# Hybrid streaming layer: where the HGRN mixer's diagonal products stand, and gates that read PSUM directly

## The chip, the cores and the metric

One core of a Trainium2 chip runs the whole kernel. The metric is the device time of one execution in microseconds. The core's engines work side by side, each with its own queue in order: TensorE (PE) multiplies matrices into PSUM, VectorE (DVE) and ScalarE (ACT) read PSUM and SBUF, GpSimd (POOL) works on SBUF only in this kernel, and SyncE (SP) issues nearly all DMA transfers. An instruction that waits holds up everything behind it in its queue.

## What is computed

One layer of a streaming encoder: RMSNorm, one input projection, three mixers on its columns (RG-LRU, SSD, HGRN), an output projection, and a SwiGLU block, for 1152 rows (1024 of a prompt, 8 x 16 of running streams). The change touches the HGRN mixer, the gate of the SSD mixer and the projections that feed both. Cut to these:

```python
h = rmsnorm(x, p["norm1_w"])                       # a scale per row, times a weight per column
proj = jnp.einsum("btd,de->bte", h, p["w_in"])     # ..., z, ..., q, fpre, ig, og

def ssd_mixer(z, ...):
    v = (y.reshape(b_, t, B_WIDTH) * jax.nn.silu(z)).reshape(b_, t, B_GROUPS, -1)
    v = v * lax.rsqrt(jnp.mean(v * v, axis=-1, keepdims=True) + EPS)
    return v.reshape(b_, t, B_WIDTH) * norm_w

def hgrn_chunk(s, inp):
    q, lf, k, v = inp
    bc = jnp.cumsum(lf, axis=1)
    decay = jnp.exp(jnp.where(causal_mask, bc[:, :, None] - bc[:, None], -jnp.inf))
    att = jnp.einsum("bthk,bshk,btshk->bths", q, k, decay)
    o = jnp.einsum("bths,bshv->bthv", att, v) + jnp.einsum("bthk,bhkv->bthv", q * jnp.exp(bc), s)
    ...

def hgrn_mixer(q, fpre, ig, og, s0, lb, norm_w):
    q = jax.nn.silu(q)
    ...
    o = o * lax.rsqrt(jnp.mean(o * o, axis=-1, keepdims=True) + EPS) * norm_w
    return o * jax.nn.silu(og), s_t
```

On the diagonal of `att` (t = s) the decay is 1, so that entry is the sum over k of q times k, per head.

## The kernel before

The rows are nine tiles of 128 (`NT`), in three chunks of 384 (`NCHUNK`). The projections take the normalised input without its row scale: the scale `rstd1` (per row, as a column) or `rrow` (the same as a row) is multiplied in when a result leaves PSUM. Every fp32 product is made of three matmuls (`mm3`, lines 144 to 146) of a high and a low half, so a tile of a projection with eight steps of depth is 24 matmuls. Channel-major projections (`ch_tile`: `f0`, `f1`, `q0`, `q1` and those of the other mixers) give tiles of 128 x 384; row-major ones (`tok_piece`: `v` with `dt`, the output gate `og`, the gate `z`) give 128 x 264 or 128 x 256 for each of the nine row tiles.

PSUM has eight banks in four tags: `a` 2, `b` 2, `c` 3, `d` 1. Row-major projections use tag `a`; `v` alternates between `a` and `b`. A bank is taken again when its last reader is through.

In `proj_f` and `proj_q` the HGRN mixer's inputs are made for both channel halves j: `bc` is the running sum of log f (a scan on DVE, line 415), `ct` is exp of the key's logarithm, and `kb` keeps `ct` and exp(bc). With q ready, `bc` becomes exp(bc) times q (line 430) and goes to DRAM (`qkbd`), and `ct` becomes k times q (line 433), from which nine small matmuls with the head selector `hsel` (128 x 2) make the diagonal `pd`, copied to `dia` (line 437). `mix_c` reads `dia` when it makes the output of a row tile, and reads the rest back from `qkbd` as `ldq`; `W` are its decay weights. The softplus of `dt` (`spt`) has one power on POOL (line 636).

A gate (`proj_gate`) is a copy of PSUM to SBUF with the row scale on ACT (line 458), a tanh of that on ACT (459), and a product on DVE (460): sg (1 + tanh(sg / 2)), which is 2 silu. It is written to DRAM and read back by the mixers. The factor 1/2 is put back through `hnw` (line 859) for `og` and in `mix_b` (line 766) for `z`.

Program order in the code is `first_tiles` (f0, f1, q0), `proj_f`, `proj_q(0)`, `proj_vdt`, `proj_q(1)`, `proj_og`, `ssd_steps`, the nine `mix_c`, then the other mixers. It isn't the order on the engines: a scheduler places the instructions of every engine by its own estimate of times, with priorities (`feed()` goes ahead by 3000), and so the matmuls of different tiles mix. Each engine then runs its list in order. Names in the rows below have the tile's number behind them, as in `ptv_4`.

Of the kernel before, what the change touches and what calls it, by code (L numbers as in the profile page):

```python
# [11 lines left out]
F32 = mybir.dt.float32  # L12
# [3 lines left out]
AF = mybir.ActivationFunctionType  # L16
ALU = mybir.AluOpType

P = 128
# [5 lines left out]
NT = NCHUNK * TPC  # L25
# [65 lines left out]
def hybrid_step(ctx, tc, xT, xTp, vec, rows, nrow, wch, wtk0, wtk1, wout, wgate, wup, wdown,  # L91
# [3 lines left out]
    V, S, G, T = nc.vector, nc.scalar, nc.gpsimd, nc.tensor  # L95
# [29 lines left out]
    rstd1 = cp.tile([P, NT], F32, name="rstd1")  # L125
    rrow = cp.tile([P, NTOK], F32, name="rrow")

    def bank(tag, name, shape):
        n = int(np.prod(shape))
        t = ps.tile([P, 512], F32, tag=tag, name=name, bufs=PB[tag])  # L130
        v = t[:, 0:n]
        if len(shape) == 2:
            v = v.rearrange("p (a b) -> p a b", b=shape[1])
        elif len(shape) == 3:
            v = v.rearrange("p (a b c) -> p a b c", b=shape[1], c=shape[2])
        return v

    def mm(out, lhsT, rhs, start=True, stop=True):
        T.matmul(out, lhsT, rhs, start=start, stop=stop)
# [34 lines left out]
    def rstd_from(out, ss, n):  # L174
        V.tensor_scalar(out, ss, 1.0 / n, EPS, ALU.mult, ALU.add)
        powc(out, out, 0)
# [5 lines left out]
    pr = p1.__enter__()  # L182
# [5 lines left out]
    hnw = pr.tile([P, 2], F32, name="hnw")  # L188
    seqm = cm[:, M_SEQ:M_SEQ + NB]
    hsel = cm[:, M_HS:M_HS + 2]  # L190
    dtb, dsk = rw[:, 0:8], rw[:, 16:24]
    st = {}
# [82 lines left out]
    def first_tiles(names, ws):  # L275

        outs = [stile(name) for name in names]
        for c in range(NCHUNK):
            hT, cs = st["hT", c], slice(c * CH, (c + 1) * CH)
            for name, w, out in zip(names, ws, outs):  # L280
                pm = bank("aabbccc"[pcount[0] % 7], f"pm{name}_{c}", [CH])
                pcount[0] += 1
                for k in range(KD):
                    mm3(pm, wk(w, k, P), (hT[:, 0, k, :], hT[:, 1, k, :]), k == 0, k == KD - 1)
                with feed():
                    if name == "q0":
                        V.scalar_tensor_tensor(out[:, cs], pm, 0.5, rrow[:, cs], ALU.mult, ALU.mult)
                    else:
                        V.tensor_tensor(out[:, cs], pm, rrow[:, cs], ALU.mult)
        return outs  # L290
# [132 lines left out]
    def proj_q(j, q):  # L423

        th = pr.tile([P, NB * 19 + 3 + 1024], F32, tag="raw", name=f"th{j}")[:, 0:NTOK]
        S.activation(th, q, AF.Tanh)
        V.scalar_tensor_tensor(q, th, 1.0, q, ALU.add, ALU.mult)
        to_tiles(qkbd[:, :, j * P:(j + 1) * P], q)
        k, eb = st["kb", j]
        V.tensor_tensor(eb, eb, q, ALU.mult)  # L430
        to_tiles(qkbd[:, :, (6 + j) * P:(7 + j) * P], eb)

        V.tensor_tensor(k, k, q, ALU.mult)
        pd = bank("b", f"pd{j}", [NT, 2])
        for t in range(NT):
            mm(pd[:, t, :], k[:, t * P:(t + 1) * P], hsel)
        V.tensor_copy(dia[:, :, 2 * j:2 * j + 2], pd)

    def proj_vdt():
        w = [load_w(wtk0[h], 1056, f"t0{h}") for h in range(2)]  # L440
# [11 lines left out]
    def proj_gate(w, name, dst, ts=range(NT)):  # L452

        for t, pm in tok_piece(w, 256, name, ts):
            sg = pr.tile([P, 256], F32, tag="stg", name=f"gs{name}{t}", bufs=2)
            th = pr.tile([P, 256], F32, tag="th", name=f"th{name}{t}", bufs=2)
            with feed():
                S.activation(sg, pm, AF.Copy, scale=rstd1[:, t:t + 1])
                S.activation(th, sg, AF.Tanh, scale=0.5)
                V.scalar_tensor_tensor(sg, th, 1.0, sg, ALU.add, ALU.mult)  # L460
                dma(dst[t], sg)

    def proj_og():
        w = [load_w(wtk1[2, h], 1024, f"t3{h}") for h in range(2)]
        proj_gate(w, "og", vod[:, :, 256:512])
# [21 lines left out]
    def mix_c(t):  # L487
# [80 lines left out]
        for h in range(4):  # L568
            j, r = h // 2, (h % 2) * 64
# [25 lines left out]
        else:  # L595
            pn = bank("c", f"pnc_{t}", [2, 64])
            for h in range(4):
                j, r = h // 2, (h % 2) * 64
# [13 lines left out]
        ss = pr.tile([P, 1], F32, tag="ssc", name=f"ssc{t}", bufs=2)  # L612
        S.activation(ke.rearrange("p j s -> p (j s)"), of, AF.Square, accum_out=ss)
        rstd_from(ss, ss, 256)
        V.scalar_tensor_tensor(of, of, ss, og, ALU.mult, ALU.mult)
        pm = bank("d", f"pmc{t}", [2, P])
        for j in range(2):
# [59 lines left out]
    def mix_b(t, last):  # L677
# [12 lines left out]
        zt = wk6[1][:, 0:512]  # L690
# [72 lines left out]
            G.tensor_tensor(yv, yv, xq, ALU.add)  # L763
        V.tensor_tensor(yv, yv, py, ALU.add)
        yf = yv.rearrange("p h d -> p (h d)")
        V.scalar_tensor_tensor(yf, yf, 0.5, zt, ALU.mult, ALU.mult)
        ss = pr.tile([P, 2], F32, tag="ssb", name=f"ssb{t}", bufs=2)
        jk = xq.rearrange("p h d -> p (h d)")
        for g in range(2):
# [86 lines left out]

    V.tensor_scalar(vc[:, V_CWB:V_CBB + 8], vc[:, V_CWB:V_CBB + 8], 0.5, None, ALU.mult)

    V.tensor_scalar(hnw, hnw, 0.5, None, ALU.mult)
    cvp = pr.tile([P, 10, 3], F32, name="cvp")  # L860
    h0t = pr.tile([P, 2, NB], F32, name="h0t")
    dma(h0t, h0)
# [24 lines left out]
    for a in zw:  # L887
        G.memset(a, 0.0)
    dtr = pr.tile([P, NH], F32, name="dtr")
    sml = pr.tile([P, 6, NH], F32, name="sml")  # L890
    etb = pr.tile([P, NB, 8], F32, name="etb")


    f0, f1, q0 = first_tiles(("f0", "f1", "q0"), ws)
    proj_f((f0, f1))
    proj_q(0, q0)
    proj_vdt()
    proj_q(1, plain_tile(13, "q1"))
    proj_og()
    ssd_steps()  # L900
    for t in range(NT):
        mix_c(t)
# [528 lines left out]
```

## Time and profile before

| | us |
|---|---|
| three runs, median (lowest to highest) | 1468.39 (1464.24 to 1470.4) |
| profiled execution | 1464.5 |
| its span, first to last instruction | 1462.7 |
| PE busy | 1364.8 |
| DVE busy | 1084.1 |
| ACT busy | 533.3 |
| POOL busy | 516.9 |

The profile is one execution. The profiled one is 3.9 us below the median of the three runs. An engine's busy time counts the time in which it has an instruction at work; what it does not count are its waits, and those of PE, the fullest engine, are the ones to look for.

### The profile page before, as it was taken

To read this page: it belongs to the slowest core of one execution; us is meant where nothing else is said; L and a number is where in the kernel's file an instruction comes from. 1 tells how busy PE (TensorE), PEld (TensorE's weight loads), DVE (VectorE), ACT (ScalarE), POOL (GpSimd) and SP (SyncE) were. 2 spreads that over 40 slices of the span, in tenths; PEclk is the share of its full clock that TensorE was granted. 3 is DMA by queue.
4 is the path that set the end of the run, shared out by engine and by line. 5 is a ranking of instruction groups with operands and counts; after the bars stand their busy time and mean duration, and the time that the engine had idled before them with its cause. 6 is when DMAs were issued, how large, how long until landed. Compare 5 with 4: busy or idle time off the path is not lost.

```text
span 1462.7 us, 24412 instructions
## 1 busy us (share of the span) xinstructions
PE 1364.8 (93%) x9341; PEld 1312.8 (90%) x9341; DVE 1084.1 (74%) x2010; ACT 533.3 (36%) x922; POOL 516.9 (35%) x417
## 2 busy tenths in 40 slices
PE   8879998999999899878799999999999999999986
PEld 7879887899988788778799999999999999998985
DVE  8555588987779588698646665556756688999996
ACT  7323265444543244364322312322222363333322
POOL 4213032100014322213644545445545432543453
PEclk9989999999999899998899999999999999999999
DMA  6245123332447686851323222233231454544523
GB/s 234 79 140 164 41 74 97 109 108 91 146 159 270 215 287 223 282 169 60 129 81 115 101 101 77 72 111 115 88 113 52 141 175 130 177 141 118 177 65 130
DMA packets 107289, 195.82 MB, mean 134 GB/s; under 512 B 10844, under 2 KB 66596, under 8 KB 107044
## 3 DMA queue, kind: packets, MB, share of 16 engines
q1 hardware_dynamic: 102276, 186.40, 38.8%
q0 software_dynamic: 4896, 7.87, 1.9%
q8 instruction: 73, 1.20, 0.3%
q14 instruction: 44, 0.36, 0.1%
HBM read 137.82 MB, written 56.41 MB: 133 GB/s over the span
## 4 chain that ended last, share of the span: by engine, by line
PE 40%; DVE 7%; DMA 1%; issue 1%; ACT 1%; POOL 0%; DVEq 0%; POOLq 0%; ACTq 0%
PE pd L146 3%; PE pd L144 3%; PE pd L145 3%; PE pS_g L144 3%; PE pS_u L144 3%; PE pS_g L146 3%; PE pS_u L145 3%; PE pS_g L145 3%; PE pS_u L146 3%; PE pA_u L144 2%; PE pA_u L146 2%; PE pA_u L145 2%; PE pA_g L145 2%; PE pA_g L144 2%; PE pA_g L146 2%; DVE as L180 1%
## 5 line engine op out<-in xcount | busy, mean ns | idle before, releaser
L144 PE MATMUL pd<-e,as 128*128 128x256 f32 (+1 forms) x560 | 167.6, 301 | 8.3 <-ACT as L179 4.9
L146 PE MATMUL pd<-e,as 128*128 128x256 f32 (+1 forms) x560 | 162.7, 298 | 3.0 <-DVE as L180 3.0
L145 PE MATMUL pd<-e,as 128*128 128x256 f32 (+1 forms) x560 | 165.1, 296 | 0.0
L144 PEld LDWEIGHTS pd<-e,as 128*128 128x128 f32 x560 | 106.5, 190 | 12.6 <-ACT as L179 6.4
L180 POOL TENSOR_TENSOR al_u<-wr_u,ah_u 128x1024 fp32r<-128x1024 f32 x30 | 72.1, 2403 | 117.0 <-ACT ah_u L179 117.0
L146 PEld LDWEIGHTS pd<-e,as 128*128 128x128 f32 x560 | 105.3, 190 | 4.7 <-DVE as L180 4.7
L145 PEld LDWEIGHTS pd<-e,as 128*128 128x128 f32 x560 | 106.1, 190 | 0.0
L180 POOL TENSOR_TENSOR al_g<-wr_g,ah_g 128x1024 fp32r<-128x1024 f32 x30 | 71.9, 2399 | 88.5 <-ACT ah_g L179 87.8
L179 ACT ACTIVATE ah_g<-wr_g 128x1024 fp32r<-128x1024 f32 x30 | 31.8, 1062 | 148.9 <-PE pS_u L145 80.5
L1040 POOL TENSOR_TENSOR g<-g,pt_u 128x256 f32<-128x256 f32 (+1 forms) x80 | 76.7, 976 | 20.3 <-DVE pt_u L1039 15.4
L144 PE MATMUL pw<-mT,wh_o 128*128 128x384 f32 x192 | 68.9, 362 | 8.3 <-DMA mT<-mixd 3.8
L144 PE MATMUL pS_g<-b,ah_g 128*128 128x256 f32 (+1 forms) x240 | 70.9, 296 | 2.1 <-ACT ah_g L179 2.1
L144 PE MATMUL pA_u<-b,ah_u 128*128 128x256 f32 (+1 forms) x240 | 71.0, 296 | 0.0
L145 PE MATMUL pA_g<-b,ah_g 128*128 128x256 f32 (+1 forms) x240 | 70.9, 296 | 0.0
L144 PE MATMUL pA_g<-b,ah_g 128*128 128x256 f32 (+1 forms) x240 | 70.8, 295 | 0.0
L146 PE MATMUL pA_u<-b,al_u 128*128 128x256 f32 (+1 forms) x240 | 70.8, 295 | 0.0
L146 PE MATMUL pA_g<-b,al_g 128*128 128x256 f32 (+1 forms) x240 | 70.7, 295 | 0.0
L144 PE MATMUL pS_u<-b,ah_u 128*128 128x256 f32 (+1 forms) x240 | 70.6, 295 | 0.0
L145 PE MATMUL pA_u<-b,ah_u 128*128 128x256 f32 (+1 forms) x240 | 70.6, 294 | 0.0
L145 PE MATMUL pS_g<-b,ah_g 128*128 128x256 f32 (+1 forms) x240 | 70.6, 295 | 0.0
L146 PE MATMUL pS_u<-b,al_u 128*128 128x256 f32 (+1 forms) x240 | 70.5, 294 | 0.0
L145 PE MATMUL pS_u<-b,ah_u 128*128 128x256 f32 (+1 forms) x240 | 70.4, 294 | 0.0
(726 smaller groups left out, 4810.7 us busy)
## 6 DMA issues: line engine op xcount, KB each, us to landing
wr_o<-in_dram SPq DMA_DIRECT2D x24, 512.0 KB, 4.8
wr_g<-in_dram SPq DMA_DIRECT2D x20, 512.0 KB, 3.5
wr_u<-in_dram SPq DMA_DIRECT2D x20, 512.0 KB, 3.5
wd<-in_dram SPq DMA_DIRECT2D x15, 512.0 KB, 3.9
wr_t<-in_dram SPq DMA_DIRECT2D x14, 512.0 KB, 3.7
fr<-ffd SPq DMA_DIRECT2D x11, 640.0 KB, 4.8
ffd<-g SPq DMA_DIRECT2D x10, 640.0 KB, 3.1
ffd<-g SPq DMA_DIRECT2D x10, 512.0 KB, 2.9
```

What stands on the lines that cost most here:

```text
L144: T.matmul(out, ah, bh, start=start, stop=False)
L145: T.matmul(out, ah, bl, start=False, stop=False)
L146: T.matmul(out, al, bh, start=False, stop=stop)
L179: S.activation(dst_hi, src, AF.Copy)
L180: eng.tensor_tensor(dst_lo, src, dst_hi.bitcast(F32), ALU.subtract)
L1040: G.tensor_tensor(g, g, u, ALU.mult)
```

## The change

Three things are changed. First, the diagonals: `proj_q` no longer makes them; a new function `diagonals`, called behind `proj_og`, makes all eighteen small matmuls into one bank and copies them once. In `proj_q` the product of k and q is now written ahead of the product of exp(bc) and q, and the latter goes from DVE to POOL. Second, the gates: ACT's tanh reads PSUM with half the row scale (`hr1` = `rstd1` / 2), and DVE multiplies 1 + tanh by PSUM itself. What is stored lacks the row scale. Third, the mixers bring it in: `mix_c` multiplies its own row factor `ss` by `hr1`, and `mix_b` uses `hr1` where 0.5 stood; the halving of `hnw` goes.

```diff
         k, eb = st["kb", j]
-        V.tensor_tensor(eb, eb, q, ALU.mult)
+        V.tensor_tensor(k, k, q, ALU.mult)
+        G.tensor_tensor(eb, eb, q, ALU.mult)
         to_tiles(qkbd[:, :, (6 + j) * P:(7 + j) * P], eb)
 
-        V.tensor_tensor(k, k, q, ALU.mult)
-        pd = bank("b", f"pd{j}", [NT, 2])
-        for t in range(NT):
-            mm(pd[:, t, :], k[:, t * P:(t + 1) * P], hsel)
-        V.tensor_copy(dia[:, :, 2 * j:2 * j + 2], pd)
+    def diagonals():
+
+        pd = bank("b", "pdia", [2, NT, 2])
+        for j in range(2):
+            k = st["kb", j][0]
+            for t in range(NT):
+                mm(pd[:, j, t, :], k[:, t * P:(t + 1) * P], hsel)
+        V.tensor_copy(dia.rearrange("p t (j r) -> p j t r", j=2), pd)
...
             with feed():
-                S.activation(sg, pm, AF.Copy, scale=rstd1[:, t:t + 1])
-                S.activation(th, sg, AF.Tanh, scale=0.5)
-                V.scalar_tensor_tensor(sg, th, 1.0, sg, ALU.add, ALU.mult)
+                S.activation(th, pm, AF.Tanh, scale=hr1[:, t:t + 1])
+                V.scalar_tensor_tensor(sg, th, 1.0, pm, ALU.add, ALU.mult)
                 dma(dst[t], sg)
...
         rstd_from(ss, ss, 256)
+        V.tensor_tensor(ss, ss, hr1[:, t:t + 1], ALU.mult)
         V.scalar_tensor_tensor(of, of, ss, og, ALU.mult, ALU.mult)
...
-        V.scalar_tensor_tensor(yf, yf, 0.5, zt, ALU.mult, ALU.mult)
+        V.scalar_tensor_tensor(yf, yf, hr1[:, t:t + 1], zt, ALU.mult, ALU.mult)
...
-    V.tensor_scalar(hnw, hnw, 0.5, None, ALU.mult)
...
+    V.tensor_scalar(hr1, rstd1, 0.5, None, ALU.mult)
     proj_f((f0, f1))
     proj_q(0, q0)
     proj_vdt()
     proj_q(1, plain_tile(13, "q1"))
     proj_og()
+    diagonals()
     ssd_steps()
```

The scheduler makes a new order of it. On PE, ahead of the first diagonals before (`ptv` are the tiles of v):

```order
L145 MATMUL ptv_4_729<-wl_t01_609,hT1_163 128x264
L146 MATMUL ptv_4_729<-wh_t01_608,hT1_163 128x264
L139 MATMUL pd0_590<-cm_91,ct0_553 128x2 x9
L144 MATMUL ptv_1_642<-wh_t00_602,hT0_104 128x264
L145 MATMUL ptv_1_642<-wl_t00_603,hT0_104 128x264
```

and where PE's list goes on behind `q0` now:

```order
L145 MATMUL pmq0_2_527<-hT2_206,wh_q0_137 128x384
L146 MATMUL pmq0_2_527<-hT2_206,wl_q0_138 128x384
L144 MATMUL ptv_1_632<-wh_t00_592,hT0_104 128x264
L145 MATMUL ptv_1_632<-wl_t00_593,hT0_104 128x264
L146 MATMUL ptv_1_632<-wh_t00_592,hT0_104 128x264
```

`ptv_1` stood behind `pd0`; it now follows `q0` at once, ahead of `q1`'s third chunk, and `pdia` follows in six pieces between the tiles of the output gate, from behind `ptog_1` to behind `ptog_8`.

On DVE, around the gates 3 to 5 of the output gate, before:

```order
L671 TENSOR_TENSOR dab_1302<-sml_314,cm_91 128x64
L460 SCALAR_TENSOR_TENSOR gsog3_1107<-thog3_1108,gsog3_1107 128x256
L536 TENSOR_TENSOR qw0_306<-W0_1_1321,ldq0_302 128x256 x2
L460 SCALAR_TENSOR_TENSOR gsog4_1138<-thog4_1139,gsog4_1138 128x256
L460 SCALAR_TENSOR_TENSOR gsog5_1169<-thog5_1170,gsog5_1169 128x256
```

and now:

```order
L463 SCALAR_TENSOR_TENSOR gsog3_1083<-thog3_1084,ptog_3_1058 128x256
L531 TENSOR_TENSOR W0_0_1302<-ldq0_301 128x16x8
L532 TENSOR_TENSOR W0_0_1302<-ldq0_301 128x16x8
L531 TENSOR_TENSOR W0_1_1311<-ldq0_301 128x32x4
L532 TENSOR_TENSOR W0_1_1311<-ldq0_301 128x32x4
L531 TENSOR_TENSOR W0_1_1311<-ldq0_301 128x64x2
L532 TENSOR_TENSOR W0_1_1311<-ldq0_301 128x64x2
L556 TENSOR_TENSOR ke0_1335<-ldq0_301 128x256
L577 COPY zw0_308<-ldq0_301 128x16
L577 COPY zw1_309<-ldq0_301 128x16
L463 SCALAR_TENSOR_TENSOR gsog4_1113<-thog4_1114,ptog_4_1088 128x256
```

The instructions that read `ldq0` stood two gates earlier; gate 4 is now behind them. What `ldq0` needs is made on POOL, whose list reads now (`spt1` is the power of the softplus):

```order
L412 TENSOR_TENSOR f1_317<-ct1_555,f1_317 128x1152
L431 TENSOR_TENSOR bc0_568<-bc0_568,q0_318 128x1152
L640 TENSOR_TENSOR spt1_1258<-cst_82,spt1_1258 128x72
L431 TENSOR_TENSOR bc1_577<-bc1_577,q1_864 128x1152
L323 COPY rawxa0_2336<-cvs_259 128x8x3
```

The two products with q are new there, one on either side of the power.

On DVE in the z stage, around the gate of row tile 7 (`px3`, `pB3`, `px0` are products of `mix_b` on PE, made behind `ptz0_8`), before:

```order
L766 SCALAR_TENSOR_TENSOR wb3_3_4432<-wb3_3_4432,wb3_1_4430 128x512
L164 TENSOR_TENSOR wl_o00_4807<-wr_o00_4805,wh_o00_4806 128x1024
L730 COPY zw0_309<-ws_4282 128x2x16
L460 SCALAR_TENSOR_TENSOR gsz07_4136<-thz07_4137,gsz07_4136 128x256
L730 COPY zw1_310<-ws_4282 128x2x16
```

and now:

```order
L463 SCALAR_TENSOR_TENSOR gsz06_4092<-thz06_4093,ptz0_6_4067 128x256
L778 SCALAR_TENSOR_TENSOR ws_4263<-ws_4263,ssb2_4387,nwr_94 128x256 x2
L180 TENSOR_TENSOR ws_4263<-pmb2_4394,ws_4263 128x512
L705 TENSOR_TENSOR wb3_3_4413<-px3_4420,sml_314 128x512
L706 TENSOR_TENSOR wb3_3_4413<-px3_4420,rw_93 128x512
L716 TENSOR_TENSOR wb3_4_4414<-pB3_4428,cm_91 128x256
L705 TENSOR_TENSOR ws_4263<-px0_4487,sml_314 128x512
L706 TENSOR_TENSOR ws_4263<-px0_4487,rw_93 128x512
L721 TENSOR_SCALAR wb3_2_4412<-wb3_2_4412,sml_314 128x128 x4
L463 SCALAR_TENSOR_TENSOR gsz07_4122<-thz07_4123,ptz0_7_4097 128x256
```

The gate comes earlier in the list than before, but it is now the last reader of its PSUM bank, where ACT's copy was.

## Rows read from the trace of the kernel before

**Rows 1.** The page: span, then busy time, share and instructions of each engine.

```profile
span 1462.7 us, 24412 instructions
PE 1364.8 (93%) x9341; PEld 1312.8 (90%) x9341; DVE 1084.1 (74%) x2010; ACT 533.3 (36%) x922; POOL 516.9 (35%) x417
```

**Rows 2.** PE's waits, whole span: us in total, times, longest.

```profile
PE pd L139 <- DVE ct L433: 9.1, 1, 9.1
...
PE pmq L144 <- ACT wh_q L160: 1.0, 1, 1.0
```

**Rows 3.** Timeline of PE, 57 to 114 us: start, duration, line, operands, idle before.

```profile
57.32 0.34 PE L146 MATMUL pmq<-hT,wl_q 128*128 128x384 f32 x1
...
64.02 0.28 PE L144 MATMUL ptv<-wh_t,hT 128*128 128x264 f32 x1
...
72.62 0.28 PE L146 MATMUL ptv<-wh_t,hT 128*128 128x264 f32 x1
81.95 4.00 PE L139 MATMUL pd<-cm,ct 128*128 128x2 f32 x18 [9.05 <-DVE ct L433]
...
105.47 0.34 PE L144 MATMUL pmq<-hT,wh_q 128*128 128x384 f32 x1
...
113.89 0.28 PE L144 MATMUL ptog<-wh_t,hT 128*128 128x256 f32 x1
```

**Rows 4.** Stretches 82 to 101.5 us: busy of each engine, granted clock, DMA.

```profile
82.00:86.00 4.00, 4.00 (x19) 4.00 (x20) 3.96 (x3) 0.00 (x0) 0.00 (x0) 0.50 0.92 251
86.00:90.50 4.50, 4.50 (x21) 4.50 (x22) 1.70 (x3) 1.72 (x2) 0.00 (x0) 0.50 0.90 246
90.50:101.50 11.00, 11.00 (x93) 11.00 (x92) 3.25 (x10) 0.61 (x1) 0.00 (x0) 1.00 0.41 133
```

**Rows 5.** Timeline of DVE, 71 to 86 us.

```profile
71.71 4.99 DVE L415 TENSOR_TENSOR_SCAN bc<-rst,ct 128x1152 f32<-128x1152 f32 x1
...
81.86 1.36 DVE L430 TENSOR_TENSOR bc<-bc,q 128x1152 f32<-128x1152 f32 x1
83.25 2.56 DVE L415 TENSOR_TENSOR_SCAN bc<-rst,ct 128x1152 f32<-128x1152 f32 x1
```

**Rows 6.** Timeline of POOL, three products and powers between 70 and 204 us.

```profile
70.61 8.51 POOL L412 TENSOR_TENSOR f<-ct,f 128x1152 f32<-128x1152 f32 x2 [12.46 <-DVE ct L411]
...
108.65 11.84 POOL L636 TENSOR_TENSOR spt<-cst,spt 128x72 f32<-128x72 f32 x1 [29.54 <-DVE spt L635]
...
200.50 2.70 POOL L382 TENSOR_TENSOR g<-g,ga 128x1152 f32<-128x1152 f32 x1 [0.96 <-DVE g L381]
```

**Rows 7.** Output gate: tile ptog (ns min/median/max, first and last start), timelines of PE, SyncE, DVE.

```profile
L146 PE MATMUL ptog<-wh_t,hT x72: 277/280/365, 114.1 to 141.6; 128*128 128x256 f32 x72
...
122.98 2.07 PE L139 MATMUL pd<-cm,ct 128*128 128x2 f32 x18
...
118.92 0.63 SPq L395 DMA_DIRECT2D qkbd<-bc  x1
...
127.88 0.29 DVE L528 TENSOR_TENSOR W<-ldq 128x128 f32<-128x128 f32 x1 [0.37 <-DMA ldq<-qkbd]
...
191.86 0.14 DVE L175 TENSOR_SCALAR ssc<-ssc 128x1 f32<-128x1 f32 x1
```

**Rows 8.** z stage: a stretch, DVE's gates grouped, and timelines of ACT and DVE.

```profile
413.00:488.00 75.00, 67.31 (x467) 61.64 (x466) 63.41 (x135) 30.40 (x67) 26.05 (x24) 0.95 0.62 209
...
L460 DVE SCALAR_TENSOR_TENSOR gsz<-thz,gsz x18: 407/417/1491, 386.9 to 489.7; 128x256 f32<-128x256 f32 x18
...
445.84 0.46 ACT L458 ACTIVATE gsz<-ptz,rstd 128x256 f32<-128x256 f32 x1
...
469.30 0.47 ACT L458 ACTIVATE gsz<-ptz,rstd 128x256 f32<-128x256 f32 x1
...
451.22 1.26 DVE L460 SCALAR_TENSOR_TENSOR gsz<-thz,gsz 128x256 f32<-128x256 f32 x1
...
475.38 0.41 DVE L460 SCALAR_TENSOR_TENSOR gsz<-thz,gsz 128x256 f32<-128x256 f32 x1
```

More of the change, by code (lines that the diff above doesn't have):

```diff
@@ L889, in hybrid_step @@
     dtr = pr.tile([P, NH], F32, name="dtr")
+    hr1 = pr.tile([P, NT], F32, name="hr1")
     sml = pr.tile([P, 6, NH], F32, name="sml")
```

## The prediction

> **What bounds the kernel now.** I read the page's busy table first, to see which engine is nearly full, then the waits of TensorE (PE), then the timelines of the longest wait. PE is busy for 1364.8 of 1462.7 us, 93%, and VectorE (DVE) for 74% [rows 1]. So time is won where PE stands still or runs slowly, and an edit on ScalarE (ACT, 36%) wins nothing by itself. Sorted by length, PE's waits begin with a single one of 9.1 us: `pd`, the diagonal products, waits for DVE's line 433, the product of `ct` and `q` [rows 2]. PE's timeline shows it: the last `ptv` matmul is issued at 72.62, `pd` starts at 81.95, after 9.05 us without work [rows 3]. The next `ptv` matmuls could have run then, since their weights and inputs lay ready, but they are behind `pd` in PE's queue. The stall is paid a second time: from 82 to 90.5 us the granted clock is 0.50, the lower level (1.2 GHz), and 1.00 in the stretch behind it [rows 4].
>
> **The change, part by part.**
>
> 1. Both diagonals go behind the output gate's projection. This removes the 9.05 us. It takes the first group of `pd` off the slow stretch: 18 records took 4.00 us there [rows 3] and 2.07 us at the full clock at 123 us [rows 7]; they come back later at 2.07, so 1.93 is won. In 86 to 90.5 us 21 matmuls took 4.5 us where the next stretch runs 93 in 11.0, or 0.118 each [rows 4]; 21 × 0.118 = 2.5, so 2.0 is won. The bank that `pd0` held is free, so the order puts `ptv_1` and the start of `ptv_3` in front of `q1`, where PE waited 1.0 for `wh_q` [rows 2]: 1.0 won. Sum 9.05 + 1.93 + 2.0 + 1.0 = 14.0 us.
>
> 2. What is late next in that stretch. One `ptv` tile takes (72.74 − 64.02) / 3 = 2.91 us and one `q` tile (113.89 − 105.47) / 2 = 4.21 [rows 3]. From 57.5, the end of `q0`, nine `ptv` and three `q` tiles are 26.2 + 12.6 = 38.8, with about 0.8 for the broadcast `prr`; the output gate could start at 97.1 instead of 113.89. But `ptv_6` needs the bank that `vs2` empties, and DVE does that behind the scan of `bc0`, which took 4.99 us beside POOL's line 412 and ended at 76.7 [rows 5, 6]. In the new order `prr` comes some 2.4 us later, and the DVE chain with it: `vs2` ends near 80, PE arrives at 79.6. I take 0.5 us lost, between 0 and 1.5. A little later `q1`'s second tile needs the bank that `vs7` empties, behind the scan of `bc1`: this one took 2.56 alone [rows 5], and POOL's new product of `bc0` will run beside it. Stretched like the first it costs 2.4, of which PE sees 0.9 by the same count; between 0 and 0.9.
>
> 3. The products of `bc` and `q` move from DVE (1.36 each [rows 5]) to POOL, where a 128x1152 product took 2.70 with little beside it and 8.51 / 2 = 4.3 beside the scan [rows 6]. The first is harmless: only a write to DRAM waits for it. The second is not: POOL's queue holds the power of the softplus in front of it, 11.84 us long [rows 6]. The power starts when the last `vs` is done, near 95 in the new time (DVE's queue holds the scan, `f1`, `vs7` and `vs8`), and ends near 107. `q1` is ready earlier, at 102: before, 118.92 − 1.36 − 113.89 = 3.7 us lay between the end of `q1` on PE and the start of that product [rows 3, 5, 7], and 98.5 + 3.7 = 102.2. On DVE the product would be done at 103.5; on POOL it ends at 109.5 to 111. In SyncE's queue the write of `bc1` waits for it, and behind that stand `vo1`, the read of `ldq0` and the write of gate 3; `W0` could start 9 us after that write was issued (118.92 to 127.88 [rows 7]), and that wait held gate writes that now stand elsewhere, so I use 8 to 9: 117.6 to 120. On DVE `gsog4` is queued behind `W0`, and `gsog4` now frees a PSUM bank. PE reaches `ptog_6`, which needs that bank, at 98.5 + 6 × 2.88 + 13/18 of the 4.1 us of diagonals = 118.8 (2.88 = (141.9 − 113.9 − 2.07) / 9 [rows 7]). With about 2.8 us for nine small DVE instructions and the gate the bank is free at 120.4 to 122.8. Cost 1.6 to 4 us, I take 2.5. Bounds: 0, if the landing is quicker than in the row, and 9, the whole of the row's delay.
>
> 4. The gates read PSUM. Per tile ACT loses one copy of 0.46 and DVE keeps its 0.42. That is 27 × 0.46 = 12.4 us of ACT, covered by PE, so nothing is won; and the bank, freed so far when ACT's copy ended, is now held until DVE is through. For the output gate I count that inside the 2.88 us of the tile in the other bank, but for item 3. In the z gates four of 18 tiles had DVE about 6 us behind: the copy ended at 446.30 and DVE at 452.48, at the last of the four 469.77 and 475.79 [rows 8]. In the new order `gsz07` stands behind products of `px3` and `px0`, which PE makes after `ptz0_8`, so PE meets `ptz1_6` with its bank still held: about 4.5 us of DVE work against 3.5 us of small matmuls. I take 2 us for the whole z stage, between 0 and 13 (below).
> DVE's own part of a z gate has a median of 0.417 us and reached 1.26 and 1.49 [rows 8]. The Trainium skill, GPSIMD Engine Reference, section 1. Specifications, says that GpSimd shares SBUF interfaces with VectorE and contends with DVE instructions that have two SBUF inputs. The new gate has one input in SBUF and one in PSUM; by that rule it would stay near 0.42, and the 2 us would be 1. No run here shows it yet, and the sum does not use it.
>
> 5. Small edits. `hr1` is one DVE instruction; nine products of `ss` with `hr1` cost about 0.14 each, as the row of the same size [rows 7], 1.3 us of DVE spread over 300 us, with PE's projection tiles as cover. Uncovered each would delay `pmc`, which PE never waits for long. The factor `hr1` in place of 0.5 in `mix_b` changes no instruction count. The scheduler orders everything anew up to about 720 us; behind that the order is the same but for a few swaps. I give this rearrangement 0, with ±4 us.
>
> Sum by parts: 14.0 − 0.5 − 0.9 − 2.5 − 2 = 8.1 us won. Counted over the tiles: the output gate starts at 97.1 + 0.5 + 0.9 = 98.5 instead of 113.89, 15.4 earlier; less the 2.07 that come back and the 4.5 of items 3 and 4, 8.8. I take 8.5. The profiled execution took 1464.5 us (span 1462.7), so 1456.0. The median of the three runs, 1468.39, is 3.9 higher and would make 1459.9. I predict 1458, the middle.
>
> **The rivals.**
> *No new wait.* All of items 2 to 4 at zero: 14 to 15 won, 1450 by the profiled run, 1452 on the middle scale of the forecast. For it: the scheduler knows the waits and spread `pd` over five gates. Against: POOL's queue.
> *POOL's queue costs more.* The delay of `ldq0` reaches PE with 5 to 9 us instead of 2.5, and the gain is 2 to 6: 1460 to 1464, no change that could be told. For it: 11.84 us stand before the product. Against: `ptog_6` has six tiles of time before it. A wash by rearrangement alone belongs here too.
> *The z gates hold the banks: slower.* Each of the four long tiles costs 6 less the 2.88 of the tile in the other bank, 3.1; four are 13. Each such wait can be followed by a slow stretch like that of [rows 4], 2.0 us, four are 8. 13 + 8 = 21, less the 10.5 of the other terms: 10.5 slower, 1475 by the profiled run, 1477 on the middle scale. It decides from about 18 us on. For it: DVE is busy for 63.4 of 75 us there [rows 8]. Against: the new order places the z tiles earlier and the gates nearer to them.
> *The change does not do what it says:* the first `pd` sits between `ptog_1` and `ptog_2`, so the long wait is surely gone; only a new one could take its place. No chance of its own.
>
> **How the numbers follow.** A measurement of this kernel can tell about 0.5%, 7.3 us. Forecast, 7 to 13 won: 0.47. No new wait: 0.12. POOL's queue or a wash: 0.28. Slower: 0.13. Faster 0.59, same 0.28, slower 0.13. For 8 in 10 the range has to take in the no-wait case and the wash: 1446 (1452 less 4 for the rearrangement, and run spread) to 1471 (the median of before and a little). About half of the slower case is left out.
>
> **What would show it.** In the profile of the changed kernel: the first `ptog` at 97 to 99.5 instead of 113.89; clock 1.00 from 60 to 120; no `pd` wait among PE's waits; the `bc1` scan near 5 us; POOL's second product behind the power, and DVE's `W0` at 117 to 120 with a PE gap of 1 to 3 us before `ptog_6`; in the z stage PE gaps before `ptz` with DVE's gate as releaser, 0 to 4 us together. I am wrong if the first `ptog` starts later than 103, if a `ptog` waits over 5 us, or if the lead at the first `ptog` is gone by 500 us.

## The result: 16.7 us faster, and where the lead grew

The changed kernel took 1451.84 us (median of 11 runs, 1446.0 to 1462.01), the kernel before 1468.58 (11 runs). The ratio is 0.989, interval [0.9866, 0.9914]; run again beside other kernels it was 0.9901 [0.9877, 0.9925]. The forecast of 1458 had the direction, and its range of 1446 to 1471 holds the time; of the gain it had two thirds. One execution of the changed kernel (1447.59 us, span 1445.8) gives these lines of the page; [rows 1] has those of before:

```profile
span 1445.8 us, 24385 instructions
PE 1349.6 (93%) x9341; PEld 1299.9 (90%) x9341; DVE 1082.0 (75%) x2016; ACT 523.2 (36%) x895; POOL 527.2 (36%) x419
```

The span is 16.9 shorter and PE's busy time 15.2. PE makes the same 9341 matmuls, and a matmul counts as busy for as long as it runs: nearly all of the gain is matmuls that ran at the higher clock, and not fewer waits. The mean granted clock of the execution rose from 0.965 to 0.976; (1 − clock) times the span, the time lost to the clock, fell from 51.2 to 34.7, by 16.5 us. The 9.05 us of `pd` are gone, but others came in their place: 3.75 in the output gate and 4.5 before the z tiles (both shown below), where before had no wait. Every run on record has its mean clock: over all 59 executions of before and 15 of the changed kernel the clock's loss is 55.5 and 41.2 us in the mean, and what is left of the span 1411.2 and 1410.1.

A table of leads (start of the first matmul of a stage in before, less that in the kernel, us, each from one profiled execution) tells where it came from. It has two executions of the changed kernel.

| | first ptog | first xa tile | first z tile | feed-forward | span |
|---|---|---|---|---|---|
| before, starts at | 113.9 | 143.0 | 380.7 | 646.6 | 1462.7 |
| changed | 14.9 | 7.5 | 9.3 | 18.8 | 16.9 |
| changed_again | 15.5 | 5.7 | 3.0 | 9.1 | 7.3 |
| product_on_dve | 15.6 | 8.3 | 8.3 | 14.6 | 16.7 |
| product_on_dve_again | 15.2 | 7.9 | 8.1 | 15.6 | 15.5 |
| diagonals_only | 15.5 | 12.0 | 15.0 | 19.3 | 14.6 |
| diagonals_only_again | 16.0 | 11.9 | 14.9 | 19.2 | 19.0 |
| diagonals_and_pool | 15.1 | 6.6 | 5.9 | 2.4 | 1.8 |
| gates_only | -1.3 | -3.4 | -3.3 | 7.7 | 7.2 |
| dead_op | -1.4 | -1.7 | -2.1 | -2.1 | -2.4 |
| dead_ops | -0.9 | -1.0 | -14.6 | -6.2 | -9.6 |
| diagonals_late_softplus | 15.6 | 12.5 | 3.9 | 9.2 | 10.8 |
| before_new_z_gates | -1.0 | -1.0 | -1.5 | 5.4 | 2.0 |

The two executions of the changed kernel, in one and the same order, are 9.6 us apart at the end. So a lead in one execution is worth no more than some 5 us either way behind the output gate; at the first ptog it repeats within 0.6. Between different orders the start of the first z tile compares only roughly: in dead_ops and gates_only PE does some 50 matmuls ahead of it that others do behind it.

### The profile page after: what moved, and what is told of

The parts are those of the page before. It is cut to its first block, busy times and chain, and to the rows that moved or that the text cites. A ratio compares the mean times of both kernels' runs of the same rounds, so it can differ in the third digit from the quotient of the medians.

```text
span 1445.8 us, 24385 instructions
## 1 busy us (share of the span) xinstructions
PE 1349.6 (93%) x9341; PEld 1299.9 (90%) x9341; DVE 1082.0 (75%) x2016; ACT 523.2 (36%) x895; POOL 527.2 (36%) x419
## 4 chain that ended last, share of the span: by engine, by line
PE 53%; DVE 27%; DMA 9%; issue 5%; ACT 3%; POOL 3%; SPq 0%; DVEq 0%; POOLq 0%; ACTq 0%
PE pS_g L144 3%; PE pS_u L144 3%; PE pS_u L145 3%; PE pS_g L146 3%; PE pS_g L145 3%; PE pS_u L146 3%; PE pA_u L144 2%; PE pA_u L146 2%; PE pA_u L145 2%; PE pA_g L145 2%; PE pA_g L144 2%; PE pA_g L146 2%; DVE as L180 2%; PE pmb L145 2%; PE pmb L144 2%
## 5 line engine op out<-in xcount | busy, mean ns | idle before, releaser
L1046 POOL TENSOR_TENSOR g<-g,pt_u 128x256 f32<-128x256 f32 (+1 forms) x80 | 76.9, 980 | 20.3 <-DVE pt_u L1045 15.4
```

Source lines behind the costliest of these rows:

```text
L1046: G.tensor_tensor(g, g, u, ALU.mult)
```

## The profile after, at the places the prediction named

PE's timeline at the start of the output gate and at its two waits (columns as in [rows 3]):

```profile
98.87 0.34 PE L146 MATMUL pmq<-hT,wl_q 128*128 128x384 f32 x1
99.04 0.28 PE L144 MATMUL ptog<-wh_t,hT 128*128 128x256 f32 x1
...
110.99 0.39 PE L144 MATMUL ptog<-wh_t,hT 128*128 128x256 f32 x1 [2.40 <-DVE gsog L463]
...
122.99 0.38 PE L144 MATMUL ptog<-wh_t,hT 128*128 128x256 f32 x1 [1.35 <-DVE gsog L463]
```

The wait of [rows 2] is gone and the first ptog starts at 99.04 instead of 113.89. Stretches of this kernel (columns as in [rows 4]: length, PE, PEld, DVE, ACT, POOL, granted clock):

```profile
58.00:72.00 14.00, 14.00 (x104) 13.73 (x104) 6.49 (x16) 8.54 (x8) 0.85 (x1) 1.00 0.34 110
72.00:97.00 25.00, 24.58 (x182) 24.10 (x181) 19.95 (x26) 9.46 (x9) 12.16 (x4) 1.00 0.59 169
97.00:120.00 23.00, 20.60 (x169) 20.40 (x168) 13.83 (x27) 3.90 (x6) 13.74 (x4) 1.00 0.72 240
120.00:128.00 8.00, 6.65 (x45) 6.57 (x44) 3.46 (x14) 2.59 (x7) 0.00 (x0) 0.79 0.28 95
```

Where [rows 4] has 0.50 the clock is now 1.00, up to 120 us; then, behind the waits that began at 108.6 and 121.6, its mean over 8 us is 0.79, and 0.21 x 8 = 1.7 us are lost. The lead at the first xa tile follows: 14.9 − 3.75 of waits − 1.7 − 2.07 for the diagonals that come back = 7.4; the table has 7.5.

Why the two waits? DVE, POOL and SyncE between 104 and 121 us, one fence each:

```profile
108.00 2.60 DVE L641 TENSOR_SCALAR spt<-spt 128x72 f32<-128x72 f32 x1 [1.96 <-POOL spt L640]
110.53 0.41 DVE L463 SCALAR_TENSOR_TENSOR gsog<-thog,ptog 128x256 f32<-128x256 f32 x1
...
120.81 0.29 DVE L531 TENSOR_TENSOR W<-ldq 128x128 f32<-128x128 f32 x1 [5.39 <-DMA ldq<-qkbd]
```

```profile
96.13 11.84 POOL L640 TENSOR_TENSOR spt<-cst,spt 128x72 f32<-128x72 f32 x1 [8.12 <-DVE spt L639]
107.94 2.62 POOL L431 TENSOR_TENSOR bc<-bc,q 128x1152 f32<-128x1152 f32 x1
```

```profile
104.95 6.33 SPq L464 DMA_DIRECT2D vod<-gsog  x2
111.34 1.12 SPq L496 DMA_DIRECT2D ldq<-qkbd  x2
...
113.18 0.38 SPq L395 DMA_DIRECT2D qkbd<-bc  x1
...
117.28 0.80 SPq L497 DMA_DIRECT2D ldq<-qkbd  x2
```

Read from the middle one: POOL's power ends at 107.97 and its product at 110.56. DVE's L641, the step of the softplus behind the power, waits for the power, and then its 72 elements take 2.60 us, as long as POOL's product beside it. Gate 1 (L463) is queued behind L641, and it is the last reader of the bank that `ptog_3` needs: 2.40 us on PE. SyncE's queue stands at gate 1's write until 111.28. Behind that stand reads of `ldq`, the write of `bc1` (issued at 113.18, 2.6 us after its product had ended) and the read that needs this write (L497, at 117.28; SyncE's waits have 0.4 us there for the write to land). W starts at 120.81, 7.6 us after the write was issued, gate 4 stands behind it, and the bank for `ptog_6` comes 1.35 late. So the last part of the path is the one that the prediction had; but the write was late because SyncE stood at gate 1's write, and not because the product was still at work.

The longest of PE's waits in the z stage, from 371 to 470 us, are (us in total, times, longest):

```profile
PE ptz L145 <- DVE wl_t L164: 3.1, 1, 3.1
PE ptz L144 <- DVE gsz L463: 1.4, 1, 1.4
```

One wait of 1.4 for a bank held by a gate, where the forecast had 2 and its slower rival 13. In the wait of 3.1 PE lacks no bank but the low half of a weight, which DVE makes; diagonals_only, with the old gates, has it too (2.5), and before has neither.

## The experiments

The code below names lines by the parts of the change.

**One thing undone: the product back on VectorE.**

```diff
-        G.tensor_tensor(eb, eb, q, ALU.mult)
+        V.tensor_tensor(eb, eb, q, ALU.mult)
```

> The changed kernel with one thing undone: the product of exp(bc) and q stays on VectorE. The order on the engines differs from the changed kernel only in a few rows around the output gate. Theory 'shared path': in the changed kernel a 72-element step of the softplus on VectorE took 2.60 us because POOL's product of bc1 ran beside it, and the gate of tile 1 stands behind that step; so here that step takes about 0.2 us, the wait of 2.40 us before ptog_3 falls under 0.4, the wait before ptog_6 is 1 to 3 us; time 1449 to 1452. Rival 'queue' (the prediction's: the product is late behind POOL's power, and what reads bc1 waits for it): W0 comes 2.5 us earlier than 120.8 and the wait before ptog_6 falls to 0, the wait before ptog_3 stays near 2.4; 1449 to 1451. Rival 'product is a gain': VectorE's queue is later by 1.4 us per product and the time is 1454 or more.

Measured: 1447.71, ratio 0.9858 [0.9835, 0.9881]. DVE, then POOL and SyncE:

```profile
110.06 0.21 DVE L641 TENSOR_SCALAR spt<-spt 128x72 f32<-128x72 f32 x1 [3.37 <-POOL spt L640]
110.17 0.41 DVE L463 SCALAR_TENSOR_TENSOR gsog<-thog,ptog 128x256 f32<-128x256 f32 x1
...
117.71 0.29 DVE L531 TENSOR_TENSOR W<-ldq 128x128 f32<-128x128 f32 x1 [2.96 <-DMA ldq<-qkbd]
```

```profile
97.27 12.76 POOL L640 TENSOR_TENSOR spt<-cst,spt 128x72 f32<-128x72 f32 x1 [15.19 <-DVE spt L639]
```

```profile
106.72 0.37 SPq L395 DMA_DIRECT2D qkbd<-bc  x1
110.62 0.32 SPq L464 DMA_DIRECT2D vod<-gsog  x1
...
113.32 0.58 SPq L497 DMA_DIRECT2D ldq<-qkbd  x1
```

Neither theory holds whole, and the time lies under the ranges of both. L641 fell from 2.60 to 0.21, as 'shared path' has it. But the wait before `ptog_3` stayed (2.52), because the power now ended at 110.03 and not 107.97: it started 1.1 later, as DVE's queue was longer by a product, and took 0.92 more. W came 3.1 earlier, as 'queue' has it: SyncE left gate 1's write only 0.3 us earlier, at 110.94, but the write of `bc1` now stands ahead of it, and L497 goes out at 113.32. A tile still waited 1.40, since in this order gate 3, which frees a bank, stands among the W products. Waits in the output gate: 3.9 against 3.75. What blocks `ptog_3` is the power in front of a gate, wherever the product is.

**The edits alone and in pairs.** The diagonals alone: `diagonals()` as in the change, the product of k and q written first, both products on V, old gates. Diagonals and POOL: the same with the product on G. Gates alone: before with the diff's edits to the gate, `hnw`, `mix_c` and `mix_b`.

> The kernel before with the diagonals alone moved behind the output gate; the product of exp(bc) and q on VectorE, gates through ACT's copy. Theory 'gates pay in the z stage': the changed kernel won 8.0 us up to the end of the output gate and another 9 to 11 between 370 and 490 us, where TensorE ran at the full clock; if the gates that read PSUM brought the second part, this kernel wins only the first: first ptog at 97 to 100, 1458 to 1462. Rival 'order': the scheduler's new order brought the second part, whatever the gates; then this kernel may show it too, and the time is 1448 to 1456 when the granted clock stays at 1.00 in the z stage, 1458 to 1464 when it falls there.

> The kernel before with the diagonals moved and the product of exp(bc) and q on POOL; gates through ACT's copy as before. Theory 'gates pay in the z stage': as with the diagonals alone, 1458 to 1462. Rival 'order': 1448 to 1464, by whether the granted clock falls in the z stage. The wait before the third or fourth tile of the output gate is under 1 us, since here the bank comes free with ACT's copy and not with the gate's product on VectorE.

> The kernel before with the new gates alone (tanh and product read PSUM, half the row scale brought in by the mixers); the diagonals where they were. The 9.05 us wait of pd stays in both theories, within 2 us. Theory 'gates pay in the z stage': 8 to 11 us won there, 1457 to 1461. Rival 'order': no rule; 1460 to 1475 by whether the granted clock falls in the z stage more or less than before. Rival 'banks held' (the prediction's slower case): PE gaps before ptz with the gate as releaser, together 5 to 13 us, 1470 to 1480.

Measured:

| kernel | diagonals | product on POOL | new gates | median us | ratio, interval |
|---|---|---|---|---|---|
| diagonals_only | yes | | | 1446.37 | 0.9846 [0.982, 0.9872] |
| product_on_dve | yes | | yes | 1447.71 | 0.9858 [0.9835, 0.9881] |
| changed | yes | yes | yes | 1451.84 | 0.989 [0.9866, 0.9914] |
| gates_only | | | yes | 1458.74 | 0.9946 [0.992, 0.9972] |
| diagonals_and_pool | yes | yes | | 1462.79 | 0.996 [0.9945, 0.9974] |

The diagonals, alone, win 22 us, more than the whole. The parts don't add: the gates win 10 without the diagonals, nothing with them (1446.4 to 1447.7) and 11 with diagonals and POOL (1462.8 to 1451.8); the product on POOL goes with a loss of 16 with old gates and of 4 with new ones. Nor is each step in this table an edit alone. Between the two kernels with new gates PE's lists differ in about ten rows; between the two with old gates, counted from the two programs, in about 700, more than between before and the changed kernel (about 500 in the same count). So the 16 is mostly a price of another order, or of order and product together; the same holds for every step that changes the gates (about 300 rows or more). 'Gates pay in the z stage' foretold gates_only (1458.7), missed diagonals_and_pool by 0.8 us and diagonals_only by 12 us at least; so the gates can't be the only source of what was won behind the output gate. 'Order' missed diagonals_only (by 1.6) and gates_only (by 1.3). The wait before `ptog_3` in diagonals_and_pool was 0.20, under 1 as expected; two later tiles waited 1.63 and 1.32.

One row shows why diagonals_only keeps more of its lead through the output gate (12.0 of 15.5 at the first xa tile). PE's waits from 95 to 140 us:

```profile
PE ptog L144 <- ACT gsog L462: 1.7, 2, 1.4
```

Here ACT's copy frees the bank. Gate 1 stood behind L641 in this kernel too (started at 110.38), but it held no bank, and PE lost 1.7 where the new gates lost 3.75 to 5.1.

**How much is a mere new order worth?** One dead instruction, and dead instructions in the mixers:

```diff
+    V.tensor_scalar(hr1, rstd1, 0.5, None, ALU.mult)
     proj_f((f0, f1))
...
         rstd_from(ss, ss, 256)
+        V.tensor_scalar(ss, ss, 1.0, None, ALU.mult)
```

(dead_op has the first alone.)

> The kernel before with one dead instruction added: hr1 (128x9 on VectorE) is made and read by nobody. It costs about 0.1 us of VectorE, but the scheduler sees it and lays 1512 of the 5509 rows of TensorE's list in another place. Theory 'order': the part of the gain behind the output gate belongs to no edit, the order of before is one draw among many; the time moves by 3 to 15 us, either way (1453 to 1475, not 1466 to 1470), the first ptog stays at 113 to 115. Rival 'edits': each edit brought its own part; without one the time stays at 1466 to 1471.

> As dead_op, and in each of the nine mix_c one more 128x1 multiplication by 1 on VectorE, in the place where the changed kernel multiplies by hr1. 2099 rows of TensorE's list move. Theory 'order': a second draw, different from the first, 1453 to 1475; nine such steps of 0.14 us cost nothing by themselves. Rival 'edits': 1466 to 1472.

Both counts of rows in these expectations are wrong: names carry running numbers, and these had shifted. Without them 3 rows of TensorE's list moved in dead_op and 586 in dead_ops (453 between before and the changed kernel). So dead_op is a second look at before, and only dead_ops a new draw. Measured: 1467.48, ratio 0.9991 [0.9978, 1.0005]; and 1473.36, 1.0023 [1.0004, 1.0043]. A new order, with nine small dead steps in it, moved the time by 3 to 4 us, to the slow side (0.6 to 6 by the interval). In this one draw ±4 was the right size for that term; one draw doesn't show how far another would move it.

**The changed kernel once more.**

> The changed kernel, unaltered, profiled once more. Theory 'the clock differs between executions of one order': the granted clock in the z stage (371 to 477 us), which was 1.00 throughout in the first profile, falls in this one in at least one stretch and 1.5 us or more are lost, while the waits of TensorE are the same within 1 us; the time is 1446 to 1460. Rival 'the order fixes the clock': the stretches of lower clock are the same ones as in the first profile, and none is in the z stage.

Measured: 1454.56, 0.9901 [0.9877, 0.9925]; the profiled execution took 1457.15. The waits of the output gate are 2.34 and 2.72. In the z stage the clock fell twice, at 388 and 440 us, and 3.2 us were lost where the first profile lost none: 'the clock differs between executions of one order' holds in that. Its condition of like waits holds before the z tiles (1.4 and 3.0, in the first profile 1.4 and 3.1), but not in the output gate, where they are 1.3 us longer.

**The softplus later.**

```diff
-    ssd_steps()
     for t in range(NT):
         mix_c(t)
+        if t == 0:
+            ssd_steps()
```

> The diagonals alone moved (product of exp(bc) and q on VectorE, old gates), and the softplus of dt with its power of 11.8 to 12.8 us on POOL written behind the first mix_c. In the profile with the diagonals alone the gate of tile 1 stood on VectorE behind a step that waited 3.09 us for that power, and SyncE's queue behind that gate. Theory 'power': without it W0 starts by 112 to 114 instead of 116.5, and the wait of 1.42 us in the output gate goes; 0 to 3 us won against the diagonals alone, 1443 to 1447. Theory 'order' adds a new draw to that: 1440 to 1458. Rival: the softplus is needed by the ssd steps later in time, and they now wait: 1450 or more with a wait of TensorE on pacs or pacT.

Measured: 1452.59, 0.9892 [0.9868, 0.9916]. DVE around W:

```profile
106.42 0.75 DVE L464 SCALAR_TENSOR_TENSOR gsog<-thog,gsog 128x256 f32<-128x256 f32 x2
...
114.70 0.29 DVE L532 TENSOR_TENSOR W<-ldq 128x128 f32<-128x128 f32 x1 [0.78 <-DMA ldq<-qkbd]
```

Where it was meant to act it acted: gates 0 and 1 go through at 106.42, W starts at 114.70 (116.52 with the diagonals alone), the tile's wait fell to 0.90. The whole became 6 us slower all the same, outside the range of 'power' and inside that of 'order'; the lead was 12.5 at the first xa tile and 3.9 at the first z tile. PE waited nowhere for pacs or pacT, so the rival's time is met and its cause is not. That the new order took more than the place gave is likely; the later softplus steps were not taken apart from it.

**The z gates alone, on either order.** One kernel is the changed one with ACT's copy and the old product in the z gates; the other is before with the new z gates only.

```diff
+                if name == "og":
                     S.activation(th, pm, AF.Tanh, scale=hr1[:, t:t + 1])
                     V.scalar_tensor_tensor(sg, th, 1.0, pm, ALU.add, ALU.mult)
+                else:
+                    S.activation(sg, pm, AF.Copy, scale=rstd1[:, t:t + 1])
+                    S.activation(th, sg, AF.Tanh, scale=0.5)
+                    V.scalar_tensor_tensor(sg, th, 1.0, sg, ALU.add, ALU.mult)
```

> The changed kernel with the gates of the z stage as before (ACT's copy with the row scale, 0.5 in mix_b); the output gate stays new. Every engine's list is that of the changed kernel up to the second z tile, near 374 us, and differs behind it (271 rows of TensorE, 201 of VectorE). Theory 'z gates pay': the changed kernel's gain behind the output gate comes from the z gates; 6 to 11 us slower than the changed kernel, 1459 to 1465. Rival 'head pays': the gain is that of the output gate's start, 15 us earlier, and the z gates are worth nothing: within 3 us of the changed kernel, 1449 to 1456. Rival 'banks held' (the prediction's 2 us): 2 us faster than the changed kernel, 1448 to 1452.

> The kernel before with the new gates in the z stage alone (hr1 in mix_b); output gate, diagonals and products as before. The lists are those of before up to the first z tiles, near 383 us (but for the one instruction that makes hr1), and differ behind it. Theory 'z gates pay': most of the 10 us that the gates alone won is here, 1457 to 1463. Rival 'head pays': nothing, 1465 to 1471. Rival 'banks held': 1470 to 1480, with TensorE waiting for the gate's product before ptz.

Measured: after_old_z_gates 0.9941 [0.9927, 0.9956], five runs of 1456.0 to 1460.7, median 1457.06. (A sixth, the profiled one, took 3222.8 us and is left out, so this kernel has no profile to read.) The median lies between the ranges of 'z gates pay' and 'head pays'. Against 0.989 and 0.9901 it is 6 to 7.5 us slower: the new z gates, with the order that they bring behind 374 us, pay there. before_new_z_gates: 1466.90, 1.0002 [0.9987, 1.0017]: beside the order of before they pay nothing. So the 10 us of gates_only aren't those of the z gates by themselves; whether the new output gate or the order brought them, no run separates.

The profiles say where such a gain lies. From the first z tile to the feed-forward block, with 1491 to 1496 matmuls in each, as stretches (one fence for each kernel; before, dead_op and diagonals_only with the old z gates, then changed, changed_again, product_on_dve and before_new_z_gates with the new ones):

```profile
380.66:646.56 265.90, 240.14 (x1496) 224.38 (x1495) 204.51 (x393) 110.64 (x218) 68.53 (x67) 0.94 0.70 225
```

```profile
382.72:648.61 265.89, 241.80 (x1496) 227.90 (x1495) 203.57 (x393) 110.97 (x219) 68.57 (x67) 0.93 0.70 226
```

```profile
365.68:627.26 261.58, 235.37 (x1491) 221.33 (x1491) 199.55 (x388) 109.19 (x217) 71.15 (x67) 0.95 0.72 231
```

```profile
371.36:627.78 256.42, 230.58 (x1494) 217.09 (x1492) 199.81 (x390) 103.56 (x200) 68.02 (x67) 0.98 0.72 234
```

```profile
377.67:637.45 259.78, 233.65 (x1494) 219.80 (x1492) 201.31 (x391) 103.63 (x200) 67.94 (x67) 0.97 0.70 231
```

```profile
372.41:631.93 259.52, 235.23 (x1493) 221.60 (x1492) 200.31 (x392) 103.76 (x200) 68.31 (x67) 0.95 0.72 231
```

```profile
382.14:641.12 258.98, 232.38 (x1496) 219.29 (x1496) 201.71 (x394) 104.00 (x202) 69.34 (x67) 0.97 0.71 232
```

First number behind the stretch: its length; second: PE busy. The difference of the two is PE's idle time, and it is 25.8, 24.1 and 26.2 with the old z gates, 25.8, 26.1, 24.3 and 26.6 with the new: no difference. What differs is the busy time of nearly the same matmuls, by the clock: 0.93 to 0.95 against 0.95 to 0.98, which touch. The stretch is 5.8 us shorter in the mean, 2 to 9.5 from kernel to kernel; the three other profiles with as many matmuls fit in: 261.63 and 269.46 with the old (diagonals_only_again, diagonals_and_pool), 258.38 with the new (product_on_dve_again). The two with 1445 matmuls are 257.50 with old gates (dead_ops) and 254.90 with new (gates_only). before_new_z_gates shows it in its profile, too, but that execution (1462.44) was the fastest of its twelve, and the median shows nothing.

The mean clock that is on record for each execution tells why. It splits a span in two: (1 − clock) times span is lost to the clock, clock times span is the rest, waits included. The clock is a mean over the whole span, PE's waits too, so the split is rough by a us or two. Means in us:

| kernel | z gates | executions | clock | lost to the clock | rest |
|---|---|---|---|---|---|
| before, beside the next | old | 17 | 0.958 to 0.964 | 55.6 | 1409.7 |
| before_new_z_gates | new | 12 | 0.964 to 0.971 | 47.0 | 1418.0 |
| after_old_z_gates | old | 5 | 0.963 to 0.969 | 48.6 | 1407.4 |
| changed | new | 15 | 0.967 to 0.976 | 41.2 | 1410.1 |
| diagonals_only | old | 9 | 0.966 to 0.976 | 43.3 | 1401.4 |

With the new z gates 7 to 9 us less were lost to the clock, in both orders. In the order of before the rest grew by as much; in the changed order it grew by 1 to 3 (2.7 in the table, 0.9 when each kernel is set beside its own runs of before), near the 2 that the prediction had for their waits. The diagonals alone, with old gates, lost nearly as little to the clock as the changed kernel, and 9 us less in the rest.

**Two kernels again.**

> The changed kernel with the product of exp(bc) and q on VectorE, once more, beside the same runs of before as the next kernel. TensorE's list differs from the changed kernel's in 11 rows, all between 95 and 145 us. Theory 'POOL costs': W0 near 117.7 instead of 120.8 and the end of the output gate 1 us earlier, and what follows is in step with it: ratio to before 0.984 to 0.988, that is 3 to 7 us faster than the changed kernel. Rival 'chance': the difference of the first comparison was the spread of the runs; 0.988 to 0.991. In both the clock lost between the first z tile and the feed-forward block is that of the kernels with new z gates, 4 to 13 us, and not 13 to 21 as with the old ones.

> The kernel before with the diagonals alone moved, once more, to see whether it beats the changed kernel. Theory 'the diagonals are the gain': ratio to before 0.982 to 0.987, 4 to 10 us faster than the changed kernel. Rival 'chance': 0.987 to 0.992. The clock lost between the first z tile and the feed-forward block is that of the kernels with old z gates, 13 to 21 us.

Measured: 1449.21, 0.988 [0.9854, 0.9906], and 1445.50, 0.9848 [0.9827, 0.9869]; the clock lost in that stretch, (1 − clock) times length over its two stages, is 8.2 and 13.0 us, the second at the edge of what was expected. The diagonals alone repeat: 15 runs of the changed kernel have a median of 1453.05, nine of diagonals_only 1445.50. It beats both kernels, the changed one by 7.5 us. For product_on_dve the new 0.988 lies at the edge of both its ranges. For the product the two comparisons give 0.9890 − 0.9858 and 0.9901 − 0.9880, or 3 to 5 us; the intervals overlap, so this is likely, not shown.

## Why the prediction was right, step by step

1. **The stall and its clock: right.** The first ptog at 98.5 was forecast; it came at 99.04 and 98.44. The clock is 1.00 from 58 to 120 us, and no `pd` wait is left. In the four profiles of the kernels that keep the old diagonals beside before (gates_only, dead_op, dead_ops, before_new_z_gates) the wait is 9.0 and the clock falls behind it every time; from 58 to 100 us in none of those that move them.

2. **The scan of `bc1`: wrong, harmless.** It took 2.87, not 5: POOL's product of `bc0` was through at 88.01, 0.4 us after the scan began at 87.56. The 0.9 of that term was not lost; of the 0.5 for `ptv_6`, 0.31 was.

3. **POOL's queue: one wait of two, and half of the path.** Forecast was 2.5 before `ptog_6`, with bounds of 0 and 9; there 1.35 was lost in one profile and 2.72 in the other. W at 117 to 120 was forecast and came at 120.81 and 121.47, 7.6 and 9.0 us after the write of `bc1` was issued, where the forecast had 8 to 9. What SyncE stood at before that write was another thing: gate 1's write, and gate 1 stood behind a softplus step, which waited for the power and then for POOL's product. The same step cost the wait that the forecast did not have: 2.40 and 2.34 before `ptog_3`, which item 4 of the prediction had counted as covered by the tile in the other bank. With both, the waits were 3.75 and 5.06, with 1.7 and 3.5 of clock behind them. The prediction had asked what is queued behind POOL's power on POOL, and not what is queued behind the instruction that waits for it on DVE. That is the step that failed; product_on_dve shows that for PE's waits here it hardly matters where the product is (3.9).

4. **The gates: wrong sign in the z stage.** 2 us lost were forecast. PE waited 1.4 for a bank, and without the clock the z gates cost 1 to 3 in the changed order, so the wait was sized well. But the stretch behind the first z tile got shorter, by 2 to 9.5 us in the profiles, and the changed kernel was 6 to 7.5 faster than after_old_z_gates. The prediction counted waits and let the clock of the stretch stand, which gave back 7 to 9 us; whether the gates raise it or the order that comes with them isn't shown. DVE's part of the gate behaved as the section 1. Specifications of GPSIMD Engine Reference in the Trainium skill has it: with one input in PSUM the 18 gates took 405 to 422 ns, where before two of them reached 1.26 and 1.49 us [rows 8], beside products on POOL.

5. **The rearrangement: 0 ± 4.** One draw by dead instructions cost 3 to 4. This term, the clock in the z stage, and item 3 are what separates 16.7 from the forecast's 8.5 to 10. By parts: at the first xa tile the lead was 7.5 and 5.7, where the forecast's terms make 15.4 − 2.07 − 2.5 = 10.8, and the rest of the 16.7 came behind it, where the forecast had expected to lose 2.

So the head of the forecast was right for its reasons, and the sum in part by luck: 3 to 5 us too much up to the first xa tile, and a gain behind it that no term had. Taken apart, the diagonals with their order are worth 22 (the forecast had 14.0 − 0.5), POOL's product likely costs 3 to 5 in one order and came with 16 in another, and the new gates gain 10, 11 or nothing, each time with a new order. Why diagonals_only keeps a lead of 15 up to the z stage, while product_on_dve has 8 there, is only half explained: 3.7 of it lies in the output gate, in waits for banks that the new gates hold and the clock behind them; the rest is another order between 130 and 370 us that was not taken apart. Open, too, is what raises the clock with new z gates, and why the same gates cost 8 us without the clock in one order and 1 to 3 in the other. Diagonals alone with new z gates was not tried.

## What to carry to other kernels

Moving work that waits out of a full engine's queue won its wait and the slow stretch behind it, and up to the first tile behind it the gain could be forecast within a microsecond. How much of it reaches the end could not: that went by the waits and the clock of what follows. An edit that rides along (work handed to a slower engine, a bank held longer) is to be timed alone: here one of them likely cost more than it saved, and the smallest version was the fastest. And when the scheduler lays the list anew, a pair of kernels times the edit together with its order: count the rows that moved before giving the edit the difference. When an instruction waits for a long one on another engine, look at what is queued behind the waiter, and at every queue that waits for that.

## What the runs showed of the hardware

A step of 72 elements on DVE took 2.60 us beside a product on POOL (107.94 to 110.56) and 0.21 without it, and ended when the product ended. The Trainium skill, SBUF — State Buffer, section SBUF: two separate sides, says that VectorE and GpSimd share one port pair as an exclusive lock: of a GpSimd operation and a VectorE operation in a 2-port perf mode or with two SBUF inputs, the first gets it for its whole instruction, and the other fully blocks. The row agrees, to 0.04 us, and two more profiles have the same 2.60 and 2.64; that this step, which has one input, ran in such a mode no trace shows. DVE's instructions that read PSUM beside POOL's product of `bc0` (85.33 to 88.01) kept their 0.48 us.

Two executions of one program, in one order, differ by 9.6 us; up to the feed-forward block PE's waits make about 3 of it, and the rest goes with the clock (0.976 and 0.970 granted in the mean). With 93% of the span in matmuls, the clock is a term of the sum of its own, and one profile shows one draw of it; the mean clock of every execution shows more.
